# A decoder block on one core: where the constant matmuls, c's transpose and the rows stand in TensorE's first microseconds

## Chip, core and metric

The kernel runs on one core of one Trainium2 chip. Its engines are TensorE (PE in the profile; PEld are its weight loads), VectorE (DVE), ScalarE (ACT), GpSimd (POOL) and SyncE (SP), which here only issues DMAs. The metric is the device time of one execution in microseconds (us), the median of the runs shown. The profile shows one execution, taken by the hardware profiler; its span goes from the first to the last instruction.

## The reference

One layer of a decoder block on x (1 x 512 x 1024, float32), with a conditioning vector c of 1024 numbers:

```python
mod = silu(c) @ w_ada + b_ada            # six parts of 1024: shift, scale, gate, twice
h = rms_norm(x, g_pre_mix) * (1 + scale1) + shift1
y = token_mixer(h, ...)                  # z = h @ w_in feeds a convolution branch and an attention branch
x = x + gate1 * rms_norm(y, g_post_mix)
h = rms_norm(x, g_pre_mlp) * (1 + scale2) + shift2
y = square(relu(h @ w_mlp_in)) @ w_mlp_out
x = x + gate2 * rms_norm(y, g_post_mlp)
```

Only what stands before the first use of `h @ w_in` is touched by the change: silu(c), the first pieces of mod, the norm of x and its transpose.

## The kernel before

Each large product is made of three matmuls on a high and a low part of both operands. Every weight is loaded by SP, split by ScalarE (a cast) and VectorE (a subtraction), and used by TensorE. The 512 rows of x are kept in four tiles of 128, which are scaled and then transposed to eight tiles of columns, `xnT`.

**The order is made by a planner.** `emit` (line 494) does not issue instructions. Each call of `pe`, `act`, `dve`, `pool` or `sp` records an operation (`record`, line 283) with a modelled cost, the operations it depends on, a rank and a `hurry`. `plan` (line 354) then runs a list schedule over a model of the five engines: on TensorE the ready operation with the lowest rank goes first, which is the place where it was recorded, less a boost; on the others the one with the earliest due time less its `hurry`. The order in which the model started the operations is the order in which they are issued, and each engine executes its own in that order. The model lets SP have at most eight loads under way: `landed` holds the modelled landing times, and the engine that issues is held until the eighth last of them. A load of SP into `f_arena` recorded while `plan.lag` is set counts as landing later by that lag; the lag of 3000 ns is set at line 1558, for the loads of the MLP's last part. `emit` is run up to fourteen times more, with buffers placed by the lives that the last plan gave them, and the plan with the shortest model is issued.

**The start.** In the order of recording:

- ScalarE's queue issues the load of c as eight rows of 128 (`c8`, lines 568 to 570). SP issues the four tiles of x and then the first 1 MB of w_ada in eight pieces (`ada_load`). ScalarE's queue issues the rows of b_ada and g_pre_mix (`row_loads`, lines 618 to 620).
- `spin(3)` records three products of a tile of ones with itself, whose result nobody reads. Then comes c's transpose, and `spin(20)` behind it (lines 633 to 638; `plan.after` holds the twenty back until c's transpose).
- VectorE copies c's columns into `cT`, ScalarE takes a tanh, and VectorE makes silu(c) with two more operations (lines 641 to 644).
- `columns(bc, 0)` (line 659) transposes the 56 rows of b_ada and g_pre_mix on TensorE and copies them to `cols` on VectorE. GpSimd makes `b1p` and `b1g` from them in three operations (lines 661 to 665).
- For each tile of x, ScalarE takes the sum of squares, GpSimd its power of -1/2 (`rstd`), and VectorE scales the tile. Then 32 transposes on TensorE go to banks of PSUM, one bank for each tile of columns, and ScalarE copies each bank to `xnT` (lines 668 to 689).
- `ada_sums` multiplies the pieces of w_ada by silu(c), for the first piece all on TensorE; `to_columns` brings the sums into columns and adds b_ada and the gains (`mod`); `first_products` makes one tile of `h` and multiplies it by a strip of w_in, 21 matmuls for each of eight tiles.

Of the kernel before, what the change touches and what calls it, by code (L numbers as in the profile page):

```python
# [17 lines left out]
P = 128  # L18
# [47 lines left out]
KOUT, VK = False, (0,)  # L66
ADD, LATE5 = 2.6, 1
ISS = 480.0
SPIN = (3, 20)
HX, HA, HG, HC = 1.2e5, 1e5, 3e3, 1.1e5  # L70


# [113 lines left out]
class Planner:  # L186
# [96 lines left out]
    def record(self, eng, fn, a, k):  # L283
        self.args = a
        aps = [v for v in a if isinstance(v, bass.AP)]
        names = dict(k)
        outs, ins = [], []
        if "out" in names:
            outs.append(names.pop("out"))
        else:  # L290
            outs.append(aps.pop(0))
        if fn == "tensor_tensor_reduce":
            outs.append(aps.pop())
        if isinstance(names.get("accum_out"), bass.AP):
            outs.append(names.pop("accum_out"))
        ins = aps + [v for v in names.values() if isinstance(v, bass.AP)]
        o = Op()
        o.i, o.eng, o.fn, o.a, o.k = len(self.ops), eng, fn, a, k
        o.succ, o.dma, o.rank, o.hurry = [], None, len(self.ops) - self.boost, self.hurry
        o.cost, o.post = self.cost(eng, fn, outs, ins, k)  # L300
        o.lag = self.lag if fn == "dma_start" and eng == "sp" and outs[0].tensor.name.startswith("f_arena") else 0.0
        o.post += self.slack if eng == "pool" else 0.0
        if fn == "dma_start":
            b = 4
            for _, c in outs[0].ap:
                b *= c
            n = min(self.run(outs[0]), self.run(ins[0]), 4096)
            o.dma = b * (6.0 + 0.043 * n) / (16 * n) * (ADD if eng == "pool" else 1)
        deps = set()
        rd = [self.region(r) for r in ins]  # L310
        wr = [self.region(w) for w in outs]
        o.bufs = set()
        for nm, units in rd + wr:
            for sp in self.spaces:
                if nm.startswith(sp):
                    o.bufs.add((sp, self.spaces[sp].owner[units[0] // 2 if sp == "psum" else units[0]]))
        for nm, units in rd:
            lw, rs = self.last_w.setdefault(nm, {}), self.reads.setdefault(nm, {})
            for u in units:
                if u in lw:  # L320
                    deps.add(lw[u])
        o.raw = set(deps)
        for nm, units in wr:
            lw, rs = self.last_w.setdefault(nm, {}), self.reads.setdefault(nm, {})
            for u in units:
                if u in lw:
                    deps.add(lw[u])
                if u in rs:
                    deps.update(rs[u])
        for nm, units in rd:  # L330
            rs = self.reads[nm]
            for u in units:
                rs.setdefault(u, []).append(o.i)
        for nm, units in wr:
            lw, rs = self.last_w[nm], self.reads[nm]
            for u in units:
                lw[u] = o.i
                rs.pop(u, None)
        if EXCL:
            for bank in {u // 2 for nm, units in rd + wr if nm.startswith("psum") for u in units}:  # L340
                runs = self.runs.setdefault(bank, [(None, []), (None, [])])
                if runs[1][0] != eng:
                    runs[:] = [runs[1], (eng, [])]
                deps.update(runs[0][1])
                runs[1][1].append(o.i)
        deps.discard(o.i)
        if self.after is not None:
            deps.add(self.after)
        o.deps = deps
        for d in deps:  # L350
            self.ops[d].succ.append(o.i)
        self.ops.append(o)

    def plan(self):
        ops = self.ops
        pe_t = 0.0
        big = sum(o.cost for o in ops if o.eng == "pe") + TAIL
        for o in ops:
            o.dead = big
            if o.eng == "pe":  # L360
                pe_t += o.cost
                o.dead = pe_t
        for o in reversed(ops):
            lat = o.post + (2.0 * o.dma if o.dma else 0.0)
            for s in o.succ:
                q = ops[s]
                o.dead = min(o.dead, q.dead - q.cost - lat)
        heaps = {e: [] for e in self.NAMES}
        free = {e: 0.0 for e in self.NAMES}
        free["sp"] = free["act"] = 750.0  # L370
        dma_free = 0.0
        landed = [0.0] * DEPTH
        future = []

        def key(o):
            return (o.rank, o.i) if o.eng == "pe" else (o.dead - o.hurry, o.i)

        for o in ops:
            o.ndep, o.ready = len(o.deps), 0.0
            if not o.ndep:  # L380
                heapq.heappush(future, (0.0, o.i))
        order = []
        now = 0.0
        while len(order) < len(ops):
            while future and future[0][0] <= now:
                o = ops[heapq.heappop(future)[1]]
                heapq.heappush(heaps[o.eng], (key(o), o.i))
            for e in self.NAMES:
                if free[e] <= now and heaps[e]:
                    o = ops[heapq.heappop(heaps[e])[1]]  # L390
                    o.t0 = now
                    free[e] = now + o.cost
                    if o.dma:
                        st = max(now + 1100.0, dma_free)
                        dma_free = st + o.dma
                        o.t1 = dma_free + 1100.0 + o.lag
                        landed.append(o.t1)
                        free[e] = max(free[e], landed[-DEPTH])
                    else:
                        o.t1 = free[e] + o.post  # L400
                    order.append(o)
                    for s in o.succ:
                        q = ops[s]
                        q.ndep -= 1
                        q.ready = max(q.ready, o.t1 if (q.eng != o.eng or o.dma) else free[e] if e == "pe" else max(free[e], o.t1 - 30))
                        if not q.ndep:
                            heapq.heappush(future, (q.ready, q.i))
            nxt = [free[e] for e in self.NAMES if free[e] > now and heaps[e]]
            if future:
                nxt.append(future[0][0])  # L410
            if not nxt:
                break
            now = max(now, min(nxt)) if min(nxt) > now else now
        assert len(order) == len(ops)
        self.length = max(o.t1 for o in ops)
        return order
# [28 lines left out]
def tile_hybrid_block(  # L445
# [25 lines left out]
    def tile_of(shape, dtype, name):  # L471
        if name not in tiles:
            tiles[name] = const.tile(shape, dtype, name=name)
        return tiles[name]
# [19 lines left out]
    def emit(past, replay):  # L494
# [70 lines left out]
            pool.tensor_tensor(o, o, nhalf[:, :n], ALU.pow)  # L565


        plan.hurry = HX + 1e4
        c8 = tile_of([8, P], F32, "c8")
        act.dma_start(out=c8, in_=c[0].rearrange("(a p) -> a p", p=P))  # L570

        plan.hurry = 0.0

# [42 lines left out]
            rows.append((r, at))  # L616

        plan.hurry = HX + 5e3
        row_loads(act, 0, ("bada", b_ada), ("gpm", g_pre_mix))
        plan.hurry = 0.0  # L620
        pos4 = tile_of([NT, P], I32, "pos4")
        pos4f = tile_of([NT, P], F32, "pos4f")
# [15 lines left out]
        pb.free(bw)  # L638
        cT = tile_of([P, 8], F32, "cT")
        tmp8 = tile_of([P, 8], F32, "tmp8")  # L640
        dve.tensor_copy(cT, pb.v(bc)[:, 0:8])
        act.activation(tmp8, cT, AF.Tanh, scale=0.5)
        dve.scalar_tensor_tensor(cT, tmp8, 1.0, cT, op0=ALU.add, op1=ALU.mult)
        dve.tensor_scalar(cT, cT, 0.5, None, ALU.mult)

        cols = []

        def columns(b, i):
            r, n = rows[i]
            q = tile_of([P, 56], F32, f"cols{i}")  # L650
            pe.transpose(pb.v(b)[:, 8:8 + n], r[:n, :], ident[:n, :n])
            dve.tensor_copy(q[:, :n], pb.v(b)[:, 8:8 + n])
            cols.append(q)

        def col(nm, i=0, n=1):
            j, at = col0[nm]
            return cols[j][:, at + i:at + i + n]

        columns(bc, 0)

        b1p = tile_of([P, 16], F32, "b1p")
        pool.tensor_scalar(b1p[:, 0:8], col("bada", 8, 8), 1.0, None, ALU.add)
        b1g = tile_of([P, 8], F32, "b1g")
        pool.tensor_tensor(b1g, b1p[:, 0:8], col("gpm", 0, 8), ALU.mult)
        pool.tensor_scalar(b1p[:, 8:16], col("bada", 32, 8), 1.0, None, ALU.add)


        for t in range(NT):
# [9 lines left out]
        for k in range(KD):  # L678
# [8 lines left out]
                act.copy(xv[:, k], pb.v(b))  # L687
            pb.free(b)
        fa.free(*xt)


        hT = [pair(T) for _ in range(KD)]
# [1209 lines left out]
```

## Time and profile before

| | |
|---|---|
| median of 3 runs | 807.27 us (807.21 to 807.29) |
| the profiled execution's own time | 806.78 us |
| its span | 804.7 us |
| busy: PE, DVE, ACT, POOL | 793.2, 728.4, 480.6, 59.8 us |
| mean granted TensorE clock | 0.997 |

Each row of a timeline gives the start of a group, its duration, engine, line, operation, what it writes and reads, and how many instructions it holds; in brackets stands how long the engine had been idle and what ended that. Nearly all operations have the line of the helper that issues them (440), so groups are told apart by the names of their tiles. A matmul of the ones is two instructions. Starts of matmuls overlap the end of the one before, so the time from start to start, and not the duration of one, is what each costs in a row of them.

### The profile page before, as it was taken

Reading aid. Unit: us, or ns where it says so; the run is one execution under the profiler, and the core shown is the slowest. Engines: PE = TensorE matmul, PEld = TensorE weight load, DVE = VectorE, ACT = ScalarE, POOL = GpSimd, SP = SyncE. Lnnn points to the kernel's source line nnn. Section 1 sums busy time; section 2 is a strip of 40 time slices with the busy share of each in tenths; the row PEclk is TensorE's granted clock in tenths of the full one; section 3 lists DMA queues with packets and bytes.
Section 4 is the critical chain, followed back from the end, with each engine's and each line's share of the span. In section 5 each row is a group of like instructions: output and inputs, shape, how many; then the busy total and the mean of one; then the engine's idle time right before and its main releaser. Section 6 shows DMA issues by size and latency. Waiting matters only on the chain.

```text
span 804.7 us, 11938 instructions
## 1 busy us (share of the span) xinstructions
PE 793.2 (99%) x4408; PEld 691.4 (86%) x4408; DVE 728.4 (91%) x1011; ACT 480.6 (60%) x818; POOL 59.8 (7%) x122
## 2 busy tenths in 40 slices
PE   8999999999999999999999999999999999999996
PEld 6788988888897888888888889988998899889985
DVE  2888999999999999999996479999999978997998
ACT  4665373177786247338333268677667766777852
POOL 3001010000000000000000010001002300320023
PEclk9999999999999999999999999999999999999998
DMA  9989252130353352163995045159817940894076
GB/s 293 357 262 343 82 129 62 52 132 1 106 184 105 104 158 64 68 216 125 336 390 163 29 150 190 53 167 253 322 44 158 280 139 27 183 296 162 27 165 136
DMA packets 97371, 130.97 MB, mean 163 GB/s; under 512 B 8897, under 2 KB 65570, under 8 KB 97314
## 3 DMA queue, kind: packets, MB, share of 16 engines
q1 hardware_dynamic: 90882, 118.66, 44.7%
q0 software_dynamic: 6336, 11.54, 9.0%
q8 instruction: 34, 0.56, 0.3%
q14 instruction: 23, 0.19, 0.1%
q10 hardware_dynamic: 96, 0.03, 0.0%
HBM read 109.23 MB, written 20.97 MB: 162 GB/s over the span
## 4 chain that ended last, share of the span: by engine, by line
PE 94%; DVE 3%; ACT 2%; DMA 0%; issue 0%; DVEq 0%
PE psum L440 94%; DVE r_arena L440 2%; DVE f_arena L440 1%; ACT f_arena L440 1%; ACT r_arena L440 1%; DMA c<-in_c_dram 0%; DVEq L1897 0%; ACT mod L440 0%; ACT L492 0%; DVEq L440 0%; DVE cols L440 0%; DVE stats L440 0%
## 5 line engine op out<-in xcount | busy, mean ns | idle before, releaser
L440 PE MATMUL psum<-r_arena 128*128 128x512 f32 (+3 forms) x4024 | 747.5, 347 | 1.1 <-ACT r_arena L440 1.1
L440 PEld LDWEIGHTS psum<-r_arena 128*128 128x128 f32 x4024 | 644.3, 189 | 89.3 <-ACT r_arena L440 2.0
L440 ACT CAST r_arena<-f_arena 128x1024 fp32r<-128x1024 f32 (+5 forms) x250 | 235.6, 966 | 126.8 <-PE psum L440 96.3
L440 DVE TENSOR_TENSOR r_arena<-f_arena,r_arena 128x1024 fp32r<-128x1024 f32 (+5 forms) x260 | 276.4, 1094 | 30.3 <-PE psum L440 11.4
L440 DVE SCALAR_TENSOR_TENSOR f_arena<-f_arena,cw 128x512 f32<-128x512 f32 x240 | 165.3, 749 | 0.0
L440 DVE TENSOR_TENSOR f_arena<-f_arena 128x1024 f32<-128x1024 f32 (+3 forms) x104 | 109.2, 1069 | 2.7 <-ACT f_arena L440 2.4
L440 ACT COPY f_arena<-psum 128x512 f32<-128x512 f32 (+4 forms) x109 | 57.8, 541 | 53.2 <-PE psum L440 46.9
L440 ACT ACTIVATE f_arena<-f_arena 128x512 f32<-128x512 f32 (+3 forms) x117 | 66.7, 593 | 23.2 <-DVE f_arena L440 22.3
L440 POOL DMA_DIRECT2D y_spill<-f_arena x40 | 34.7, 867 | 263.0 <-ACT f_arena L440 259.6
L440 DVE SCALAR_TENSOR_TENSOR f_arena<-f_arena,cT 128x1024 f32<-128x1024 f32 (+2 forms) x52 | 52.7, 1021 | 0.7
L440 DVE TENSOR_TENSOR f_arena<-psum,f_arena 128x512 f32<-128x512 f32 (+1 forms) x43 | 28.5, 672 | 18.6 <-PE psum L440 15.8
L440 ACT CAST r_arena<-psum 128x512 fp32r<-128x512 f32 (+2 forms) x59 | 30.2, 551 | 17.8 <-PE psum L440 17.3
L440 DVE TENSOR_TENSOR r_arena<-psum,r_arena 128x512 fp32r<-128x512 f32 (+2 forms) x59 | 35.8, 640 | 0.3
L440 ACT ACTIVATE f_arena<-psum 128x512 f32<-128x512 f32 x35 | 20.4, 593 | 25.3 <-PE psum L440 23.7
L440 PE MATMUL psum<-ident,f_arena 128*128 128x128 f32 x234 | 32.2, 274 | 0.1
L440 PEld LDWEIGHTS psum<-ident,f_arena 128*128 128x128 f32 x234 | 26.7, 140 | 6.3 <-issue 1.3
L440 POOL TENSOR_TENSOR stats<-stats,nhalf 128x1 f32<-128x1 f32 (+1 forms) x17 | 13.2, 780 | 163.2 <-ACT stats L440 140.6
L440 ACT ACTIVATE r_arena<-psum 128x512 fp32r<-128x512 f32 x12 | 7.2, 598 | 28.8 <-PE psum L440 28.8
L440 ACT ACTIVATE r_arena<-f_arena 128x512 fp32r<-128x512 f32 (+3 forms) x21 | 13.4, 637 | 14.3 <-DVE f_arena L440 14.3
L440 POOL TENSOR_TENSOR lns<-lns,nhalf 128x4 f32<-128x4 f32 x1 | 1.4, 1396 | 246.4 <-DVE lns L440 246.4
L440 DVE CUSTOM_DVE_ANT_0 f_arena<-psum,mask 128x128 f32<-128x128 f32 (+3 forms) x32 | 15.1, 486 | 0.1
L440 DVE SCALAR_TENSOR_TENSOR f_arena<-f_arena 128x512 f32<-128x512 f32 (+1 forms) x18 | 13.2, 747 | 0.0
(97 smaller groups left out, 229.3 us busy)
## 6 DMA issues: line engine op xcount, KB each, us to landing
f_arena<-in_w_ada_dram SPq DMA_DIRECT2D x32, 512.0 KB
f_arena<-in_w_mlp_in_dram SPq DMA_DIRECT2D x32, 512.0 KB
f_arena<-in_w_mlp_out_dram SPq DMA_DIRECT2D x32, 512.0 KB
f_arena<-in_w_in_dram SPq DMA_DIRECT2D x24, 512.0 KB
y_spill<-f_arena POOLq DMA_DIRECT2D x40, 256.0 KB, 6.3
f_arena<-in_w_ada_dram SPq DMA_DIRECT2D x24, 256.0 KB
f_arena<-in_x_dram SPq DMA_DIRECT2D x8, 512.0 KB
h_spill<-r_arena SPq DMA_DIRECT2D x16, 256.0 KB
```

Of the source, the lines that this page charges most:

```text
L440: getattr(self.real[o.eng], o.fn)(*o.a, **o.k)
```

## The change

The constants before c's transpose become nine calls and those behind it eleven. The operations on c between its transpose and silu(c) get the `hurry` of x's loads. The rows' transpose, their copy and the three operations of GpSimd are recorded behind the transposes of x. In the model, the loads of ScalarE's queue can now have a lag, 1500 ns for c and 2500 ns for the rows, and a lag no longer counts for the eight loads under way; the latter also touches the loads with the lag of 3000 ns.

```diff
-SPIN = (3, 20)
+SPIN = (9, 11)
+CLAG = (1500.0, 2500.0)
...
-        o.lag = self.lag if fn == "dma_start" and eng == "sp" and outs[0].tensor.name.startswith("f_arena") else 0.0
+        o.lag = self.lag if fn == "dma_start" and (eng == "act" or outs[0].tensor.name.startswith("f_arena")) else 0.0
...
-                        landed.append(o.t1)
+                        landed.append(o.t1 - o.lag)
...
-        plan.hurry = HX + 1e4
+        plan.hurry = HX + 3e4
         c8 = tile_of([8, P], F32, "c8")
+        plan.lag = CLAG[0]
         act.dma_start(out=c8, in_=c[0].rearrange("(a p) -> a p", p=P))
+        plan.lag = 0.0
...
         plan.hurry = HX + 5e3
+        plan.lag = CLAG[1]
         row_loads(act, 0, ("bada", b_ada), ("gpm", g_pre_mix))
+        plan.lag = 0.0
...
+        plan.hurry = HX
         dve.tensor_copy(cT, pb.v(bc)[:, 0:8])
         act.activation(tmp8, cT, AF.Tanh, scale=0.5)
         dve.scalar_tensor_tensor(cT, tmp8, 1.0, cT, op0=ALU.add, op1=ALU.mult)
         dve.tensor_scalar(cT, cT, 0.5, None, ALU.mult)
+        plan.hurry = 0.0
...
-        columns(bc, 0)
-
-        b1p = tile_of([P, 16], F32, "b1p")
-        pool.tensor_scalar(b1p[:, 0:8], col("bada", 8, 8), 1.0, None, ALU.add)
-        b1g = tile_of([P, 8], F32, "b1g")
-        pool.tensor_tensor(b1g, b1p[:, 0:8], col("gpm", 0, 8), ALU.mult)
-        pool.tensor_scalar(b1p[:, 8:16], col("bada", 32, 8), 1.0, None, ALU.add)
...
         fa.free(*xt)
+
+        columns(bc, 0)
+
+        b1p = tile_of([P, 16], F32, "b1p")
+        pool.tensor_scalar(b1p[:, 0:8], col("bada", 8, 8), 1.0, None, ALU.add)
+        b1g = tile_of([P, 8], F32, "b1g")
+        pool.tensor_tensor(b1g, b1p[:, 0:8], col("gpm", 0, 8), ALU.mult)
+        pool.tensor_scalar(b1p[:, 8:16], col("bada", 32, 8), 1.0, None, ALU.add)
```

## The prediction, made before the changed kernel ran

> **What bounds the kernel now.** I read the page's chain first, then who TensorE waits for, then busy time by stage.
>
> ```profile
> span 804.7 us, 11938 instructions
> ...
> PE 94%; DVE 3%; ACT 2%; DMA 0%; issue 0%; DVEq 0%
> ```
>
> ```profile
> PE psum L440 <- DMA c<-in_c_dram: 1.9, 1, 1.9
> PE psum L440 <- ACT r_arena L440: 1.1, 2, 0.9
> PE psum L440 <- POOL ones L479: 1.0, 1, 1.0
> ```
>
> Next, busy time by stage. The columns are the stretch, its length, the busy time of PE, PEld, DVE, ACT and POOL, the granted clock, the DMA share and GB/s.
>
> ```profile
> 12.20:23.10 10.90, 10.85 (x63) 5.74 (x62) 5.34 (x10) 4.87 (x11) 2.40 (x5) 1.00 1.04 308
> 23.10:60.00 36.90, 36.02 (x173) 29.43 (x172) 30.89 (x44) 24.23 (x45) 1.02 (x6) 1.00 0.95 307
> 60.00:700.00 640.00, 639.74 (x3534) 559.44 (x3533) 596.73 (x852) 379.00 (x657) 34.05 (x45) 1.00 0.49 150
> ...
> 797.00:805.00 8.00, 0.38 (x4) 0.17 (x2) 4.52 (x10) 0.61 (x3) 1.07 (x2) 0.64 0.65 182
> ```
>
> TensorE holds 94% of the chain and stands still for 0.26 us between 60 and 700 us. Its waits add up to 4.0 us, and 1.9 of them are the wait for c. So the end is nearly "when TensorE starts its real work, plus that work, plus a tail of some 7 us on VectorE and the output DMAs". The change touches the start, so I went through the first 16 us in order of time (start, duration, engine, operation).
>
> ```profile
> 1.00 1.65 PE L440 MATMUL psum<-ones 128*128 128x128 f32 x6 [1.00 <-POOL ones L479]
> ...
> 4.58 0.24 PE L440 MATMUL psum<-ident,c 8*128 8x8 f32 x1 [1.94 <-DMA c<-in_c_dram]
> ...
> 4.76 7.61 PE L440 MATMUL psum<-ones 128*128 128x128 f32 x40
> ...
> 5.06 0.21 ACT L440 ACTIVATE tmp<-cT 128x8 f32<-128x8 f32 x1 [2.73 <-DVE cT L440]
> 5.18 1.04 ACT L440 ACTIVATE r_arena<-f_arena 128x1024 fp32r<-128x1024 f32 x1
> ...
> 7.38 0.75 DVE L440 TENSOR_SCALAR f_arena<-f_arena,stats 128x1024 f32<-128x1024 f32 x1 [1.69 <-POOL stats L440]
> ...
> 8.15 0.55 POOL L440 TENSOR_TENSOR stats<-stats,nhalf 128x1 f32<-128x1 f32 x1 [0.81 <-ACT stats L440]
> ...
> 12.29 0.27 PE L440 MATMUL psum<-ident,rows 56*128 56x56 f32 x1
> ...
> 12.49 1.48 PE L440 MATMUL psum<-ident,f_arena 128*128 128x128 f32 x9
> 12.60 0.22 DVE L440 COPY cols<-psum 128x56 f32<-128x56 f32 x1 [4.47 <-PE psum L440]
> 12.73 0.74 DVE L440 TENSOR_SCALAR f_arena<-f_arena,stats 128x1024 f32<-128x1024 f32 x1
> 12.90 0.88 POOL L440 TENSOR_SCALAR b1p<-cols 128x8 f32<-128x8 f32 x2 [4.21 <-DVE cols L440]
> 13.53 0.20 PEld L440 LDWEIGHTS psum<-ident,f_arena 128*128 128x128 f32 x2 [0.29 <-DVE f_arena L440]
> ...
> 13.90 1.46 PE L440 MATMUL psum<-f_arena,cT 128*1 128x256 f32 x6
> 13.92 1.38 POOL L440 TENSOR_TENSOR stats<-stats,nhalf 128x1 f32<-128x1 f32 x2
> ...
> 14.52 1.58 DVE L440 TENSOR_SCALAR f_arena<-f_arena,stats 128x1024 f32<-128x1024 f32 x2 [1.04 <-POOL stats L440]
> ```
>
> The first big product, on a weight of w_in, is this one:
>
> ```profile
> 23.10 0.47 PE L440 MATMUL psum<-r_arena 128*128 128x512 f32 x1
> ```
>
> Three things are to be seen in the first sixteen microseconds. x's first tile was scaled at 7.38 + 0.75 = 8.13 us, yet its transposes start at 12.49, behind 40 matmuls on constants and the transpose of the rows. The second tile's factor was ready at 8.15 + 0.55 = 8.70, but its scaling on VectorE stood behind the copy of the rows' columns, which waits for that same transpose: it ran at 12.73. GpSimd stood 4.21 us before b1p for the same reason, and the third and fourth tile's factors queued behind it until 13.92. So the constants and the rows hold up everything that follows.
>
> **The change, part by part.** Each call of the constant product issues two matmuls: before 6 + 40, after 18 + 22. Their pace has two values, though the granted clock is printed as 1.00 throughout this stage.
>
> ```profile
> 4.76 6.13 PE L440 MATMUL psum<-ones 128*128 128x128 f32 x27
> ```
>
> ```profile
> 10.68 1.69 PE L440 MATMUL psum<-ones 128*128 128x128 f32 x13
> ```
>
> ```profile
> L440 PE MATMUL psum<-ones 128*128 128x128 f32 x16 | 3.6, 421 | 0.0
> ```
>
> ```profile
> L440 PE MATMUL psum<-f_arena,cT 128*1 128x256 f32 x24 | 5.8, 378 | 0.0
> L440 PE MATMUL psum<-ident,f_arena 128*128 128x128 f32 x32 | 5.0, 285 | 0.1
> ...
> L440 PE MATMUL psum<-ones 128*128 128x128 f32 x2 | 0.4, 275 | 0.0
> ```
>
> The first 27 of the 40 come every (6.13 - 0.42) / 26 = 0.22 us, the last 13 every (1.69 - 0.28) / 12 = 0.118 us (0.42 and 0.28 are single durations, since starts overlap the one before). The pace changed at 10.68, which is 6.1 us after TensorE began to run without a gap (4.58).
>
> *Constants and c.* After: 18 matmuls from 1.00 at 0.22 us end at 4.96. c is there at 4.45 (0.13 us before its transpose at 4.58), so the 1.94 us wait goes, and what is late next is the last constant, by 0.5 us. c's transpose takes 4.76 - 4.58 = 0.18, to 5.14. TensorE now runs without a gap from 1.00, so by the trace's 6.1 us the pace changes at 7.1. Until then (7.1 - 5.14) / 0.22 = 9 of the 22 are done, and the other 13 take 1.5 us: the constants end at about 8.65, and x's first transposes start at 8.7 instead of 12.49, **3.8 us** earlier. [...]
>
> *c's operations.* The higher due-time credit puts the copy, the tanh and two products at the head of VectorE and ScalarE when ready: about 0.5 us later than now, with c's transpose. In before, x's first square (5.18) stood behind the tanh (5.06). If it still does, x's first tile is scaled at 8.6, and if the planner, now told that c lands 1.5 us later, lets it go first, below 8.13. Both are covered by the constants until 8.7, so I cost it at nothing; without that cover it is 0.5 us.
>
> *Rows behind x's first tile.* Seven transposes fit the free banks of PSUM. Nine took 1.48 us with a wait of 0.29 among them, so one takes (1.48 - 0.29 - 0.28) / 8 = 0.11; seven end at 9.5, and the rows' transpose goes at 9.5 instead of 12.29, 2.8 us earlier. Behind it are queued, on VectorE, the copy and the second tile's scaling, and on GpSimd b1p, b1g and two factors. They keep their offsets (second tile's scaling +0.44, its transposes 13.53 - 12.29 = +1.24), so the second tile is transposed at 10.75 and the fourth is scaled at 16.1 - 2.8 = 13.3. Against before, the first tile's 0.8 us has moved ahead of the rows, so between 9.7 and 10.75 TensorE has no transpose: it idles unless the first products of c with w_ada fill in. No DMA moves in SP's queue; the ACT queue's three small loads keep their order.
>
> ```profile
> 0.00:5.00 5.00, 2.06 (x8) 1.77 (x9) 0.14 (x1) 1.58 (x2) 2.75 (x43) 1.00 0.58 216
> 5.00:10.00 5.00, 5.00 (x24) 5.00 (x25) 1.12 (x4) 4.77 (x11) 1.11 (x2) 1.00 1.08 354
> 10.00:15.00 5.00, 4.95 (x34) 3.67 (x32) 1.36 (x3) 0.77 (x3) 2.10 (x5) 1.00 1.12 310
> ```
>
> 1.08 MB land by 5 us and 2.85 MB by 10. x is 2.10 MB, so the first 128 KB pieces of w_ada come from about 8.3 us and the last of eight at 11. They could fill the hole. In before the first of these products (13.90) stood behind the second tile's first transposes (13.53).
>
> *The sum.* Nothing filled in: 2.8 us. All filled: 3.8. The trace bounds it below by zero only if a later stage gives it back (below). I take **3.0**, near the order that before shows. The work between the rows and the first big products, 12.2 to 23.1, is 10.85 of 10.90 us TensorE, so an earlier start moves all of it. The profiled execution took 806.78 us, 2.1 over its span; less 3.0 that is 803.8. It lies 0.5 below the median of the runs, so on the median 807.27 - 3.0 = **804.3 us**.
>
> *The planner.* Every order is made anew. Besides, landings with an extra lag no longer hold back the modelled SP queue; that lag stands on the loads of the last stage. I cost that at nothing, as TensorE stands still there for nearly nothing, and keep it as a rival.
>
> **The rivals.** *The lead is eaten on VectorE.* Chain and stages:
>
> ```profile
> 158.61 3.63 DVE f_arena L440 x8
> ...
> 184.19 47.78 PE psum L440 x271
> ```
>
> ```profile
> 80.00:100.00 20.00, 20.00 (x128) 20.00 (x127) 20.00 (x29) 7.42 (x13) 0.00 (x0) 1.00 0.28 92
> 100.00:200.00 100.00, 99.79 (x503) 85.02 (x502) 99.55 (x182) 56.83 (x122) 2.55 (x1) 1.00 0.26 76
> ```
>
> From 80 us on VectorE is as full as TensorE, and the chain runs mostly over it from 158.6 until TensorE takes over at 184.2. If its queue is not 3 us earlier there, TensorE waits for it, and 0.4 us of gain is left: 806.9. Against it: VectorE idles 36.9 - 30.9 = 6 us between 23 and 60 waiting for results of the same stage, so it moves with TensorE.
>
> *The rows aren't put where the code records them,* since the planner sorts by its own ready times. Rows ahead of x: the rows go at 8.7, 3.6 us earlier, so 803.7. Little apart.
>
> *Slower: weights late.* The looser SP model issues loads in another order.
>
> ```profile
> SPq L440 <- DVE r_arena L440: 379.8, 101, 28.1
> ```
>
> SP waits in order, up to 28.1 us for one buffer, and a load put behind such a wait comes late by it. A 512 KB load (0.524 MB) takes 1.5 us at the 354 GB/s of the stretch from 5 to 10 us. Three loads late by 1.6 each are 4.8 us on TensorE: 807.27 - 3.0 + 4.8 = 809.1. It decides from 3.0 + 1.6 = 4.6 us of new stalls after 60 us, where before has under one between 60 and 700. The DMA share there, 0.49, speaks against it.
>
> *The clock falls back.* If transposes and small products don't keep the fast pace, the stage from 8.7 runs at 0.22 instead of 0.118: its 32 transposes and 24 products, some 9 us, could cost 7 more, 811.3. Before ran the same mix from 12.49 to 23.1 at the fast pace (32 transposes, mean 285 ns). [...]
>
> **Chances.** Forecast 0.65 (802.6 to 805.6); rows elsewhere 0.05, also faster; eaten 0.18; weights late 0.09; clock 0.03. Faster by over 0.2% (1.6 us, about what a measurement here can tell from no change) 0.70, within 0.18, slower 0.12. The low end is 3.8 plus the 0.9 us wait for ACT, if that goes too: 807.27 - 4.7 = 802.6. The high end takes in the eaten lead, to 807.4; the slower cases stay outside.
>
> **What would show it.** Right: no wait for c; the pace changes near 7 us; x's first transposes at 8.5 to 9, the rows right behind them; the first big product (23.10 in before) at 20 to 20.5; the same tail. Wrong: x's first transposes early but the first big product at 22 or later (the hole was not free), or a wait of TensorE for VectorE near 180 us as long as the lead, or new waits for loads after 500 us.

## The result, and the profile after

| | before | after |
|---|---|---|
| median of 10 runs each | 807.02 us | 804.49 us |
| lowest and highest | 805.95, 807.29 | 803.68, 806.44 |
| the profiled execution | 806.78 us | 804.19 us |
| its span | 804.7 us | 802.4 us |

The ratio is 0.9977, with a 95% interval of 0.9967 to 0.9987: faster by 2.5 us, where 3.0 were forecast (804.3). Six of the ten runs after lie between 803.7 and 804.6 and four between 805.9 and 806.4, which widens the interval; the section on the hardware shows what one run of the upper kind looks like. In the profiled executions the time outside the span fell too, from 2.1 to 1.8 us; no run shows why.

Of the page after, the span and the chain by engine; then, of its view of waits, for whom TensorE waited (total, times, longest):

```profile
span 802.4 us, 11926 instructions
...
PE 87%; DVE 9%; issue 2%; ACT 1%; DMA 1%; DVEq 0%; POOLq 0%; POOL 0%
```

```profile
PE psum L441 <- ACT r_arena L441: 1.1, 2, 0.9
PE psum L441 <- ACT f_arena L441: 1.0, 1, 1.0
PE psum L441 <- POOL ones L480: 1.0, 1, 1.0
```

The wait for c (1.9 us) is gone, and a wait of 1.0 us for something that ScalarE writes into `f_arena` is new. The chain's smaller share for TensorE is no loss by itself: the chain now runs over VectorE in several stretches, but the view of waits has no wait of TensorE for VectorE.

The first microseconds of after, in order of time:

```profile
1.00 4.21 PE L441 MATMUL psum<-ones 128*128 128x128 f32 x18 [1.00 <-POOL ones L480]
...
5.14 0.27 PE L441 MATMUL psum<-ident,c 8*128 8x8 f32 x1
...
5.34 3.12 PE L441 MATMUL psum<-ones 128*128 128x128 f32 x22
...
6.75 0.76 DVE L441 TENSOR_SCALAR f_arena<-f_arena,stats 128x1024 f32<-128x1024 f32 x1 [0.49 <-POOL stats L441]
...
8.11 0.75 DVE L441 TENSOR_SCALAR f_arena<-f_arena,stats 128x1024 f32<-128x1024 f32 x1 [0.60 <-POOL stats L441]
...
8.29 0.93 PE L441 MATMUL psum<-ident,f_arena 128*128 128x128 f32 x7
...
9.15 0.26 PE L441 MATMUL psum<-ident,rows 56*128 56x56 f32 x1
...
9.25 0.55 POOL L441 TENSOR_TENSOR stats<-stats,nhalf 128x1 f32<-128x1 f32 x1 [1.18 <-ACT stats L441]
...
9.35 0.44 PE L441 MATMUL psum<-ident,f_arena 128*128 128x128 f32 x2
9.45 0.22 DVE L441 COPY cols<-psum 128x56 f32<-128x56 f32 x1 [0.59 <-PE psum L441]
...
9.78 0.90 POOL L441 TENSOR_SCALAR b1p<-cols 128x8 f32<-128x8 f32 x2
...
18.99 0.48 PE L441 MATMUL psum<-r_arena 128*128 128x512 f32 x1
```

c's transpose comes without a wait at 5.14, x's first tile is transposed at 8.29 (12.49 before) and the rows behind it at 9.15. The second tile is scaled on VectorE at 8.11, ahead of the copy of the rows' columns (9.45), and its transposes follow at 9.35 (13.53 before). The first big product starts at 18.99 in place of 23.10: a lead of **4.1 us**, over the forecast's 3.0.

The end of the span is only 2.3 us earlier, so some of the lead is lost on the way. Both programs issue the same 4024 big products in `psum<-r_arena`. From the two traces I take the start of the n-th and subtract:

| product | start before, us | lead of after, us |
|---|---|---|
| first | 23.10 | 4.11 |
| 1001st | 240.18 | 4.04 |
| 1401st | 340.24 | 4.06 |
| 1501st | 365.73 | 2.61 |
| 3401st | 693.28 | 2.60 |
| last | 797.1 | 2.42 |

So 1.45 us are lost between 340 and 366 (1.24 of them by the 1451st product), and 0.2 near 700, which was not followed. Here is the place, in the timeline of after and then of before (SPq is SP issuing a load):

```profile
341.19 0.38 SPq L441 DMA_DIRECT2D f_arena<-in_w_conv_out_dram  x1
...
346.49 1.05 ACT L441 CAST r_arena<-f_arena 128x1024 fp32r<-128x1024 f32 x1 [1.17 <-DMA f_arena<-in_w_conv_out_dram]
347.44 0.47 ACT L441 ACTIVATE f_arena<-psum,lns 128x256 f32<-128x256 f32 x1
347.81 0.19 ACT L441 ACTIVATION_READ_ACCUMULATOR f_arena<-psum,lns 128x1 f32 x1
347.90 0.58 ACT L441 ACTIVATE f_arena<-psum 128x512 f32<-128x512 f32 x1
...
348.06 0.44 PE L441 MATMUL psum<-ident,f_arena 128*128 128x128 f32 x2 [1.01 <-ACT f_arena L441]
```

```profile
325.33 0.38 SPq L440 DMA_DIRECT2D f_arena<-in_w_conv_out_dram  x1
...
344.97 1.06 ACT L440 CAST r_arena<-f_arena 128x1024 fp32r<-128x1024 f32 x1 [4.12 <-PE psum L440]
```

Before, the first large load of w_conv_out is issued at 325.33, and ScalarE's cast of it waits for TensorE only. After, the same load is issued at 341.19, and the cast stands 1.17 us for it. Behind the cast on ScalarE stand an activation of a result in PSUM (347.44, its sum read at 347.81) and a copy out of PSUM (347.90). TensorE's transposes start at 348.06, as the activation's sum has been read (347.81 + 0.19 = 348.00) and before the copy has ended: the activation held up by the cast is TensorE's new wait. SP's order has changed: before, three loads of w_ada stand in a row ahead of this load, after, six.

### The profile page after: what moved, and what is told of

Its sections match the earlier page's. It is cut to its first block, busy times and chain, and to the rows that moved or that the text cites. A ratio compares the mean times of both kernels' runs of the same rounds, so it can differ in the third digit from the quotient of the medians.

```text
span 802.4 us, 11926 instructions
## 1 busy us (share of the span) xinstructions
PE 791.8 (99%) x4402; PEld 689.0 (86%) x4402; DVE 730.0 (91%) x1011; ACT 482.8 (60%) x818; POOL 60.2 (7%) x122
## 4 chain that ended last, share of the span: by engine, by line
PE 87%; DVE 9%; issue 2%; ACT 1%; DMA 1%; DVEq 0%; POOLq 0%; POOL 0%
PE psum L441 87%; DVE f_arena L441 5%; DVE r_arena L441 4%; ACT r_arena L441 1%; DMA f_arena<-in_w_conv_out_dram 1%; ACT f_arena L441 0%; DVEq L1904 0%; POOLq L1904 0%; ACT mod L441 0%; POOL stats L441 0%; POOL ones L480 0%; DVE stats L441 0%; DVEq L441 0%; DVE lns L441 0%; POOLq L1895 0%
```

## The experiments

Two theories of the lost 1.5 us. A: the new order of the later stage loses it, whatever the lead. B: VectorE, full from 80 us on (in before busy for 20.00 of the 20.00 us to 100, and 99.55 of the 100 behind them), lets only some 2.6 us of lead through. In all experiments "lead" is as in the table above. Where the order of before or after is kept, the planner runs as it did there, and only what is issued of the constants differs, or a few named operations are held back. Each ratio is against runs of before made together with that experiment.

All leads are against the one trace of before, in which TensorE's pace changed at 10.82 us by the clock record. In the other traces it changed between 4.02 and 8.78; in all of them that is 3.0 to 6.2 us after the start of an unbroken run of matmuls (10.82 - 4.58 = 6.2 in before, 6.19 - 1.00 = 5.2 in after). A microsecond at the slow pace instead of the fast one costs the constants about 1 - 0.118 / 0.22 = 0.46 us, an estimate from the two paces of before. So leads at the first big product, the 4.1 of after among them, can differ by up to about 1 us for this alone; a loss from one product to a later one doesn't depend on it.

**Eighteen constants behind c in after's order** (a_9_18). The planner's order is issued with 9 and 18 calls (`spins` holds the numbers of the constants' operations; the lines that fill it are left out):

```diff
+        want = [9, 18]
         for o in order:
+            g = 0 if o.i in self.spins[:SPIN[0]] else 1
+            if o.i in self.spins:
+                n, want[g] = want[g], 0
+                for _ in range(n):
+                    getattr(self.real[o.eng], o.fn)(*o.a, **o.k)
+                continue
             getattr(self.real[o.eng], o.fn)(*o.a, **o.k)
```

> The changed kernel with its own order on every engine, but eighteen constant products behind c's transpose in place of eleven: 14 more matmuls at 0.112 us, so all of TensorE's work starts 1.56 us later. Theory A (the new order itself loses 1.5 us near 345 us, whatever the lead): first big product at 20.55, last matmul at 796.2, time 806.0. Theory B (VectorE lets only some 2.6 us of lead through there): first big product at 20.55, but no wait for ScalarE near 345, last matmul at 794.7 and time 804.5 as before the edit.

805.87 us (11 runs), ratio 0.9992 (0.9983 to 1.0001). Lead 2.88 at the first big product, 2.78 at the 1351st, 0.97 at the 1501st, 0.68 at the last. The lead shrank by 1.2 and the loss stayed (1.81): A.

**Six constants behind c** (a_9_6): the same edit with `want = [9, 6]`.

> The changed kernel with its own order, but six constant products behind c's transpose: the constants end 1.1 us earlier, near 7.2, and x's first tile is scaled at 7.51, so x's transposes start near 7.6 in place of 8.29. A: the first big product and the end come up to 0.7 us earlier, time 803.8 to 804.5. B: the first big product comes earlier, the end does not, 804.5. If the clock opens later because fewer constants run, both are 1 us worse.

804.84 us (9 runs), 0.9979 (0.997 to 0.9989). x's first transposes came at 7.72, but the first big product at 18.93, only 0.06 earlier than in after's profile. TensorE's pace also changed 0.8 us later in this run (6.96 against 6.19 by the trace's clock record); how much that took was not separated. What came late next is in the trace:

```profile
9.77 1.02 PE L449 MATMUL psum<-f_arena,cT 128*1 128x256 f32 x4 [0.25 <-DMA f_arena<-in_w_ada_dram]
```

c's first product with w_ada, at 9.83 in after, waits for its load here, so in this run an earlier end of the constants could bring little more. The end was not earlier; the loss between the 1351st and the 1501st product was 2.06 here. Neither theory's forecast was met, as the first big product did not come earlier.

**Nine and eleven in before's order** (b_9_11): the same edit of the kernel before, with `want = [9, 11]`.

> The kernel before with its own order on every engine, but nine constant products ahead of c's transpose and eleven behind it. A: the start gains 3.5 to 4.1 us, nothing is lost near 345, time 803.2. B: the lead over 2.6 us is lost between 300 and 350, time 804.5. If the change's new place of the rows makes the gain, this kernel gains under 3 at the first big product.

803.40 us (5 runs), 0.9961 (0.9948 to 0.9973). Lead 3.46 at the first big product and 3.38 at the last. Almost nothing is lost on the way, over VectorE or elsewhere: B falls.

**Three and twenty in after's order** (a_3_20): `want = [3, 20]` in the changed kernel.

> The changed kernel with its own order, but three constant products ahead of c's transpose and twenty behind it, as before the change. The wait for c is back and the constants end near 12.2. Lead at the first big product 0 to 0.6 us. A: the loss near 345 stands, time 808.0. B: no loss there, time 806.8.

808.14 us (11 runs), 1.0015 (1.0006 to 1.0023). Lead 1.34 at the first big product (x's first transposes at 11.16, ahead of the rows; I had expected at most 0.6), -0.65 at the 1501st, -0.93 at the last. The pace changed at 8.78 here and at 10.82 in before's trace; by the estimate above some 0.9 us of the lead is that, and not the order. With before's constants, the new order of the later stage is slower than the kernel before.

**After's first microseconds, before's order behind them** (b_start). The edit of b_9_11, and three holds on before's order (the code that holds operations back is left out; numbers are those of the recorded operations: c's tanh and two products; the rows' transpose, copy and GpSimd's three operations; on the right what must be issued first):

```diff
+        holds = [({40, 41, 42}, {48}),
+                 ({43, 44, 45, 46, 47}, {59, 64, 69, 74, 79, 84, 89, 94}),
+                 ({45, 46, 47}, {54})]
```

> Before's order everywhere, but the first microseconds in the changed kernel's order: nine and eleven constant products, x's first square ahead of c's tanh, x's first tile ahead of the rows. Theory A (the loss near 345 us belongs to the new order of the later stage): lead 4.1 us at the first big product and at the last matmul alike, time 802.9. Theory B (VectorE lets only 2.6 us through): 804.5. If the place of the rows is worth nothing, it equals the kernel with the constants alone, 803.4.

802.54 us (5 runs), 0.9952 (0.994 to 0.9964): the lowest median of the study, though its interval overlaps that of b_9_11. Lead 4.39 at the first big product, 4.35 at the last.

**ScalarE's cast behind the copies** (a_cast), in after's order:

```diff
+        holds = [({3027}, {2935, 2744})]
```

> The changed kernel, but ScalarE's cast of the first piece of w_conv_out, which waits for its load near 345 us, stands behind the two next operations of its queue. If TensorE stood there because ScalarE's copies out of PSUM queued behind that cast, the wait of 1.0 us and most of the 1.5 us lost go: last matmul near 793.4, time 803.1. If the load itself is what TensorE needs, nothing changes, 804.4.

803.29 us (5 runs), 0.9961 (0.9949 to 0.9973). In its view of waits:

```profile
PE psum L458 <- ACT r_arena L458: 1.1, 2, 0.9
PE psum L458 <- POOL ones L497: 1.0, 1, 1.0
PE psum L458 <- issue: 0.6, 1, 0.6
PE psum L458 <- DVE f_arena L458: 0.2, 1, 0.2
```

TensorE's wait for ScalarE's write into `f_arena` is gone; the lead is 4.57 at the 1351st and still at the 1451st product. A wait of 0.6 remains at 355, and with it 0.8 of the 1.45 us are lost there instead (3.77 at the 1501st). The view doesn't name its cause; in the timeline the products that end it, at 355.53, read tiles that VectorE makes from 355.15 on, out of a result of GpSimd that ends at 354.79. So the cast in ScalarE's queue made the stop near 347, and the late load was not itself what TensorE needed then. The median fell by 1.2 us; of the loss along the trace only 0.65 went (1.45 to 0.80). The pace changed at 4.15 in this profile and at 6.19 in after's, so the two leads are not to be compared as they stand.

**Both lags at zero** (a_nolag):

```diff
-CLAG = (1500.0, 2500.0)
+CLAG = (0.0, 0.0)
```

> The changed kernel with both modelled lags at zero. Its order differs from the changed kernel's in the first microseconds alone: the rows' transpose and copy go ahead of x's first tile, and c's tanh ahead of x's first square. Lead at the first big product 3.4 to 3.6 us (as with the constants alone in before's order), and the 1.5 us near 345 are lost as in the changed kernel: time 805.0.

806.27 us (12 runs), 1.0002 (0.9993 to 1.0011), against 805.0 expected. The order puts the rows' copy on VectorE ahead of x's first scaling, and b1p on GpSimd ahead of the second factor: in its profile x's first transposes wait 0.97 us for that scaling and the second tile's another 0.82, as before the change but with a shorter queue of constants. The lead at the first big product is 1.52 (3.4 to 3.6 were expected) and by the 201st it is gone. The loss near 345 is there, 1.66. This profile is of an execution of 808.70 us, in which the clock also falls back twice (at 10.85 and at 34.74, below); the waits for the scaling come before that, and the other nine runs, 805.8 to 807.3, miss the forecast too.

**The line on the lag undone** (a_landed):

```diff
-                        landed.append(o.t1 - o.lag)
+                        landed.append(o.t1)
```

> The changed kernel with one line undone: a modelled lag counts again for the eight loads under way. Its first microseconds are in the changed kernel's order on every engine; in SP's queue the first large load of w_conv_out stands behind three loads of w_ada, as before the change, and not behind six. If that line made the loss near 345 us: lead at the first big product 4.1 to 4.4 us, the same at the last matmul, no wait of TensorE for ScalarE's copy, time 802.5 to 802.9. If the loss comes with any early start, 804.4.

803.62 us (5 runs), 0.9961 (0.9947 to 0.9974). Lead 3.82 at the first big product, 3.70 at the 1451st: the loss near 345 is gone. But 0.2 go by the 1501st and 0.5 by the 2001st, at a new wait:

```profile
PE psum L441 <- ACT r_arena L441: 1.1, 2, 0.9
PE psum L441 <- POOL ones L480: 1.0, 1, 1.0
PE psum L441 <- DVE f_arena L441: 0.5, 1, 0.5
```

The last matmul keeps 2.92. The time is 0.7 over the top of the expected range: the profile shows these small stops, and a pace that changed at 7.01, so that x's first transposes came at 8.68.

**The constants alone, planned anew** (b_spin): the kernel before with `SPIN = (9, 11)`.

> The kernel before with the constants at nine and eleven, and the order made anew by the planner. SP's queue has the order of the kernel with that one line undone. Lead at the first big product 3.3 to 3.5 us, no loss near 345, time 803.4, as with the constants changed in before's own order. If a new order costs a microsecond by itself, 804.5.

805.19 us (11 runs), 0.9987 (0.9978 to 0.9996): a miss, 1.8 over the 803.4 expected. In the timeline of its start:

```profile
8.77 0.27 PE L440 MATMUL psum<-ident,rows 56*128 56x56 f32 x1
9.07 0.22 DVE L440 COPY cols<-psum 128x56 f32<-128x56 f32 x1 [2.81 <-PE psum L440]
9.21 0.74 DVE L440 TENSOR_SCALAR f_arena<-f_arena,stats 128x1024 f32<-128x1024 f32 x1
...
10.01 0.99 PE L440 MATMUL psum<-ident,f_arena 128*128 128x128 f32 x7 [0.97 <-DVE f_arena L440]
...
10.40 2.21 POOL L440 TENSOR_TENSOR stats<-stats,nhalf 128x1 f32<-128x1 f32 x3
```

GpSimd had made x's first factor by 9.38 - 1.46 = 7.92, but VectorE stood until 9.07, because the rows' copy is ahead of x's scaling in its queue, and GpSimd's three later factors stand behind b1p and b1g. In before's fixed order (b_9_11) the scaling is ahead of the copy. The lead at the first big product is 1.77 and at the last 0.87, with the 0.5 of a_landed lost at the same later place.

**The changed kernel again** (again1, again2, again3).

> The changed kernel once more, for one look. Its runs lie in two groups, near 804.3 and near 806.1, with granted clocks of 0.997 and 0.996. If this one falls in the upper group and the theory is right that the clock falls back for one window of 3.4 us in x's stage, the pace of TensorE shows 3.4 us at 0.22 us a step after it had been 0.11, and the first big product is 1.7 us later, near 20.7. If it falls in the lower group, first big product near 19.0 and a time of 804.3.

> The changed kernel once more, for one look: lower group 804.3 with the first big product near 19.0, or upper group 806.1 with the granted clock back at half for one window of 3.4 us, within x's stage or right behind the wait for ScalarE near 31 us, as the kernel without lags showed at 10.85 and at 34.74.

> The same kernel and the same two possibilities as the run before it: 804.3, or 806.1 with one window at half clock.

804.84, 804.67 and 806.22 us. Leads at the first big product 3.80, 3.81 and 3.69; losses between the 1351st and the 1501st product 1.72, 1.58 and 1.50. The third, the upper kind, lost another 1.63 by the 201st product, not in x's stage but behind the wait that ends at 32.41; the last section shows it. In again2 and again3, whose constants ended early, c's first product with w_ada waits 0.46 and 0.78 us for its load (10.13 and 10.25), so the early end brought no more lead.

## Why the prediction was right, point by point

That the forecast of 804.3 met 804.49 is partly luck: two of its terms were wrong in opposite directions. In the profiles the start gave 1.1 us more than the 3.0 forecast, and 1.7 of the lead were lost later, which had been put at nothing. The way the gain comes about was right.

- **The wait for c and the constants: right.** The wait went. Constants were to end so that x's first transposes start at 8.7; they started at 8.29, and at 8.70, 8.18 and 7.97 in the three repeats. The pace changed 5.2 us after TensorE's start in the profile of after, not the 6.1 that I had carried over from before; in all traces it was 3.0 to 6.2.
- **c's operations at nothing: right.** They ended before 6.3, and the first tile was scaled by 7.51, under cover of the constants. That credit and the new place of the rows in the code did nothing of their own: planned without either, the order is the same on every engine (by the planner's order; such a kernel was not run). The order of the first microseconds comes from the constants and the modelled lags.
- **"They keep their offsets": wrong, the mis-sized term.** The forecast left the second tile's scaling and GpSimd's factors behind the rows' copy and b1p, moved as they stood, and so had TensorE idle from 9.7 to 10.75. The planner, told that the rows land late, put the second scaling ahead of that copy and the third factor ahead of b1p. The hole closed, and the lead at the first big product was 4.1 (3.7 to 4.1 in four profiles) instead of 3.0. Some 0.4 of the difference is the pace, with which x's first transposes came at 8.29 instead of 8.7; in again1 they came at 8.70, and the lead was 3.80, the forecast's figure with everything filled in. The forecast had the first piece of w_ada at 8.3; in three profiles TensorE waited for it until 9.77, 10.13 and 10.25 (a_9_6, again2, again3).
- **The rows elsewhere: wrong price.** With the rows ahead of x this rival had 3.6 us gained, little apart from the forecast. In b_spin, where they go first, VectorE's copy of them held up x's scaling, and the lead was 1.77; in a_landed, whose pace changed at the same time (7.01 against 7.00) and where x goes first, it was 3.82. So the rows behind x's first tile are worth some 2 us in a new order; in before's fixed order, where VectorE scaled x's first tile ahead of the copy anyway, they are worth at most 0.9 (b_start 4.39 against b_9_11 3.46), of which a part is the pace, which changed at 4.04 in the one and at 5.22 in the other.
- **The planner at nothing: wrong.** The new order costs 1.45 us between 340 and 366 and 0.2 near 700. The rival named this mechanism, a load put behind others in SP's order, and put its price at three times 1.6 us; one load was late, it stopped ScalarE, and TensorE lost about 1.5. What made it is the line on the lag, which I had read as harmless because TensorE stood still for nearly nothing in the stage whose loads carry that lag: with that line undone the loss near 345 goes (a_landed), with the lags of c and the rows at zero it stays (a_nolag), and without that line it doesn't arise either (b_9_11, b_start, b_spin). The prediction had looked for the line's effect in the stage that carries the lag, and not in the loads ahead of it. How the line reaches a load that is issued well ahead of the stage where the lag is set, through fourteen plans and the buffers' lives, was not followed.
- **Lead eaten on VectorE: false.** Leads of 3.4 and 4.4 us pass through the stretch up to 350 us almost whole (b_9_11 3.44 to 3.37, b_start 4.40 to 4.34). VectorE was as full as in before (busy for 596.5 and 596.0 of the 640 us from 60 to 700, against 596.7), but what it works on came earlier too. The range had been stretched to 807.4 for this rival, whose own price was 806.9.
- **The clock falls back: seen in one of the four profiles of the changed kernel,** again3, at another place (32.83) and for one stretch of 3.41 us at 0.50, which cost 1.63 us.

## What to carry to other kernels

Where one engine is the chain for 94% and almost never stands still (in before 0.26 us between 60 and 700 us), a microsecond saved at its start reaches the end as long as the order behind it stays (3.38 of 3.46 us in b_9_11, 4.35 of 4.39 in b_start); check that it does by subtracting the starts of the same instruction in both traces along the program, since an end that moves by about the right amount can hide a gain and a loss. When an order is made by a planner, an edit of its model is an edit of the whole order: keep the order fixed and change one thing in what is issued, to tell the two apart. Here the first microseconds of the change on the old order gave 802.5 us, 0.48% under before, where the change itself gave 0.23%.

## What was not expected of the hardware

In again3, the profiled execution of 806.22 us, the granted clock fell to half for one stretch of 3.41 us, although TensorE had stood still for a single wait, of 0.87 us, in the stretch before it (columns as before; the clock is the third number from the end):

```profile
29.42:32.83 3.41, 2.54 (x16) 1.79 (x15) 3.26 (x5) 2.67 (x7) 0.41 (x1) 1.00 1.11 349
32.83:36.24 3.41, 3.41 (x10) 2.63 (x9) 3.06 (x5) 1.63 (x3) 0.12 (x1) 0.50 1.08 370
```

The wait of 0.87 us for ScalarE's split of h, which every one of these kernels has once (it ends between 31.4 and 36.1 us), lies inside the first stretch; the second runs at 0.50 and costs the 1.63 us. The same wait did not do so in again2, where the stretch had the same busy time:

```profile
29.85:33.26 3.41, 2.54 (x14) 1.92 (x14) 2.99 (x5) 3.25 (x8) 0.40 (x1) 1.00 1.08 348
33.26:36.67 3.41, 3.41 (x16) 2.82 (x16) 3.29 (x6) 1.08 (x2) 0.12 (x1) 1.00 1.07 371
```

And in the profile of a_nolag, with longer holes in x's stage:

```profile
7.44:10.85 3.41, 1.62 (x11) 1.08 (x10) 1.98 (x4) 3.31 (x9) 2.41 (x5) 1.00 1.12 311
10.85:14.26 3.41, 3.41 (x9) 0.86 (x9) 1.16 (x2) 0.00 (x0) 0.74 (x1) 0.50 0.93 283
```

No run shows what makes the clock fall. The stretches of one clock that begin and end within a trace are whole multiples of 3.413 us (one of them at half clock in the rows of again3 and a_nolag above; of full clock 788.48 us or 231 in before, 791.89 us or 232 in after). Counted in such steps from the instant at which the clock record first has full clock (10.82 in before, 6.19 in after), ten of the fourteen traces have the whole wait in one step, with TensorE busy 2.52 to 2.54 us of it each time. Half clock followed in two, again3 and a_nolag (31.33 to 34.74), and full clock in eight, so the busy time alone doesn't decide. The two that fell hold six big products and eight short ones on the tile of ones beside the wait, where seven of the eight others hold at least seven big and at most five short ones; but the step of a_cast, 28.04 to 31.45, holds the same six and eight and was followed by full clock. What decides is open. A fall of this kind fits the four upper runs of the changed kernel (granted clock 0.995 to 0.996, where the other six have 0.997 or 0.998), but they left no trace.
